# Turning token rows by DMA instead of on TensorE, with the norm's gains folded into the weights, in a hybrid SSD and RWKV-7 decoder layer

## The chip, the cores and the metric

The kernel runs on one core of one Trainium2 chip (trn2). The metric is the device time of one execution in microseconds. The core's engines each run their own queue of instructions: TensorE (PE in the profile, its weight loads PEld), VectorE (DVE), ScalarE (ACT), GpSimd (POOL) and SyncE (SP), which here only issues DMAs. An instruction waits at the head of its queue for the semaphores it needs, and everything behind it waits too.

## What is computed

One decoder layer over 2048 tokens of width 1024, in float32. Two groups of heads read the same normalised input:

```
xn   = RMSNorm(x) * pre_mix_norm
proj = xn @ w_in                       # 1024 -> 1544 (SSD) + 1792 (RWKV-7)
y_ssd, y_rwkv = ssd_mixer(...), rwkv7_mixer(...)
h = x + RMSNorm([y_ssd ; y_rwkv] @ w_out) * post_mix_norm
y = h + RMSNorm(ConvGLU(RMSNorm(h) * pre_ffn_norm)) * post_ffn_norm
```

The RWKV-7 mixer mixes each projected column with that of the token before (weight `mu`), forms a decay, keys, receptances and values, and runs a recurrence over tokens on a 64x64 state for each of eight heads:

```
sa = S @ a_t
S  = S * w_t + sa b_t^T + v_t k_t^T
y_t = S @ r_t
```

The SSD mixer passes its 1024 conv columns through a causal convolution of four taps, and does a chunked scan with chunks of 128 tokens.

## The kernel before

Three phases follow one another, each overlapping the next at its end: phase_R (the dense projections of RWKV-7 and of the SSD conv columns, the conv, and the RWKV-7 recurrence), phase_S (the SSD scan, the output projection, the first residual) and phase_F (the gated feed-forward network). The change lies nearly all in phase_R, with small parts in phase_S.

Phase_R works through 16 blocks of 128 tokens. The weights stay in SBUF for the whole phase: 14 tiles of 128 columns for RWKV-7 (`wr`) and 8 for the conv columns (`wc`). Each weight is scaled by 256 and split into a high and a low half of 16 bits (`load_w`, lines 280 to 295); the pattern SPLITS names who does it: "A" ScalarE or "G" GpSimd for the high half, "V" VectorE for the low one. The normalised tokens are split in the same way. A dense step (`dense`, line 210) is then 24 matmuls: eight slices of the 1024 inputs, and for each high by high, high by low and low by high.

Tokens arrive with tokens on the partitions, and the matmuls need them with the 1024 inputs on the partitions. The step `load` (line 312) does this for the next block. It has two halves. The first loads 512 KB of rows (`xin`), squares and sums them on ScalarE (line 190), forms the inverse root on GpSimd (lines 181, 182) and scales the rows on ScalarE (line 192). Each half then calls `flip_rows` (line 195): four TensorE transposes of 128x128 float32 into one PSUM bank (line 201), a VectorE multiply that empties the bank and applies `pre_mix_norm` (line 203), a ScalarE copy to the high half (line 206), and a VectorE subtraction for the low half (line 207). The bank has the tag "pt" with one buffer (in block 0 it is a buffer of "ms"). The result `xt` also goes to DRAM (`XN`, line 324) for phase_S.

The other steps of a block that the text names:

- `d.0` to `d.13` and `conv.0` to `conv.7`: the dense steps (lines 341 and 360), with what empties their PSUM banks: ScalarE copies (lines 353 to 355, 370), VectorE mixing (line 357), and for the conv a GpSimd bias (line 373), three taps on VectorE (line 378), a tanh and a product (lines 382, 383), and a store `XC` on SP (line 384).
- `low`, `keys`, `norm`, `receptance`: they make the decay and its cumulative sums (a VectorE scan with the mask `smask`, line 414), the keys and the scaled operands AR and BK.
- `gram.0`, `gram.1` (line 459): two sets of products of BK and AR, each into two banks of "ms", which VectorE masks into `G` (line 467). "ms" has two buffers and is shared with the small matmuls of `low`, `norm`, `transposed` and `values`.
- `solve` (line 471): the inverse of the unit triangular 32x32 blocks of G. Four DMAs carry the blocks to DRAM (`ATd`, line 479), four bring them back with one block per partition (`atl`, line 483), a chain of 62 small dependent VectorE instructions does forward substitution (lines 492, 495), four DMAs write the result (`XTd`, line 498) and four read it in its place (`XT`, line 504). All these are on SP.
- `merge.0`, `merge.1`, then `own`, `update` and `state` for each half block of 64 tokens, `transposed`, `values`, `gate`, `finish`: the recurrence proper. `merge.0` begins with two VectorE transposes of XT (`XW`, line 536) and the matmuls `pw` (line 543).

The order of TensorE's work is written out by hand in the tables FIRST (block 0), SECOND, PLAN (blocks 2 to 14) and LAST. In them `f.` is a step of the current block, `b.` of the block before, `a.` of the one before that, and `n.` of the next; so a block's dense steps, norm, gram and solve run in one round, and its merge and recurrence in the next. Only TensorE keeps this order as written (line 1498); the instructions of the other engines are put in order when the program is built, by a schedule that takes the order of the text as priority and its own estimate of the times. In PLAN, between the two grams and the next round, the order before is:

```
... f.conv.4 b.update.0 f.receptance f.gram.0 f.conv.5
f.gram.1 n.load.0 b.state.0 n.load.1 f.conv.6 b.own.1 f.conv.7 b.update.1 f.d.10 f.solve f.d.11 ...
```

Phase_S splits the weights of its z gate in four pieces of 1024 columns (`load_wz`, line 734).

Of the kernel before, what the change touches and what calls it, by code (L numbers as in the profile page):

```python
# [17 lines left out]
D = 1024  # L18
# [11 lines left out]
NC_S = 512  # L30
COLS = (
# [23 lines left out]
class Space:  # L55
# [22 lines left out]
    "cw cb mus omu w0h a0h ka5 kam tiny vr gnv gnr ss pnv pnr", "XT0 XT1 qs S0_0 S0_1 tS ysb yln tg",  # L78
# [3 lines left out]
    "wdt dtb Ab Db cst_s sng", "wst", "ws0", "ws1", "xt", "ws2", "ws3", "dv de dq ds dtt da nac", "sz", "th", "xbc", "R",  # L82
# [55 lines left out]
def load_consts(tc, K, pool, cst, par, rows, rows16):  # L138
    nc = tc.nc
    K.cst = pool.tile([P, NCONST - NC_S], F32, name="cst")  # L140
    nc.sync.dma_start(K.cst, cst[:, 0:NCONST - NC_S])
# [4 lines left out]
    for name, (a, b) in COFF.items():  # L146
        if b <= NCONST - NC_S:
            setattr(K, name, K.cst[:, a:b])
# [37 lines left out]
def norm_rows(tc, K, work, src, sfx, junk):  # L186
# [3 lines left out]
    nc.scalar.activation(junk, src.rearrange("p (a b) -> p a b", b=P), AF.Square, accum_out=ss)  # L190
    r = rsqrt_cols(tc, K, work, ss, 1, 1.0 / D, EPS, "pn")
    nc.scalar.activation(src, src, AF.Identity, scale=r[:, 0:1])


def flip_rows(tc, K, psp, pstag, src, g, dst, col, sfx, q):

    nc = tc.nc
    ps = psp.tile([P, 4, P], F32, name=f"pt{sfx}{q}", tag=pstag[0], bufs=pstag[1])
    for u in range(4):
        kt = 4 * q + u  # L200
        nc.tensor.transpose(ps[:, u, :], src[:, kt * P:(kt + 1) * P], K.ident)
# [1389 lines left out]
```

## Time and profile before

| | us |
|---|---|
| median of three runs | 2733.22 |
| the three runs | 2723.94, 2741.75, 2733.22 |
| the profiled execution | 2723.75 |
| its span, first to last instruction | 2722.0 |
| TensorE busy | 2500.4 (92%) |
| VectorE busy | 1951.3 (72%) |
| ScalarE busy | 1209.6 (44%) |
| GpSimd busy | 1251.6 (46%) |
| mean granted TensorE clock | 0.963 of full |

Phase_R's own work fills the first 954 us or so, with TensorE busy for 865 of them, and runs out beside phase_S from there on; phases S and F fill the rest. In the timeline a line gives the start, the length, the engine, the line of the program, the operation, the tile written and the tiles read, the shapes and the number of instructions merged; in brackets stands how long the engine had been idle before and what ended the wait. SPq is SP's queue of DMA issues. In a row of grouped instructions the last part is the idle time of the engine just before them and what ended it. In a row of stretches stand the stretch, its length, and for each of the engines TensorE, weight loads, VectorE, ScalarE and GpSimd the busy time, then the granted clock, the busy share of the DMA engines and GB/s. TensorE's clock is granted in full or by half, so a stretch shows a mean between 0.5 and 1.

### The profile page before, as it was taken

To read this page: it belongs to the slowest core of one execution; us is meant where nothing else is said; L and a number is where in the kernel's file an instruction comes from. 1 tells how busy PE (TensorE), PEld (TensorE's weight loads), DVE (VectorE), ACT (ScalarE), POOL (GpSimd) and SP (SyncE) were. 2 spreads that over 40 slices of the span, in tenths; PEclk is the share of its full clock that TensorE was granted. 3 is DMA by queue.
4 is the path that set the end of the run, shared out by engine and by line. 5 is a ranking of instruction groups with operands and counts; after the bars stand their busy time and mean duration, and the time that the engine had idled before them with its cause. 6 is when DMAs were issued, how large, how long until landed. Compare 5 with 4: busy or idle time off the path is not lost.

```text
span 2722.0 us, 54074 instructions
## 1 busy us (share of the span) xinstructions
PE 2500.4 (92%) x21468; PEld 1580.4 (58%) x21468; DVE 1951.3 (72%) x3649; ACT 1209.6 (44%) x2448; POOL 1251.6 (46%) x1348
## 2 busy tenths in 40 slices
PE   5999999999999979999987999898988999999998
PEld 4888888888888845555533444343433444444443
DVE  7778788888788655667777677787789734554457
ACT  5456555556555544444544543434344333122132
POOL 5334444344444443334468664746567523222234
PEclk8899999999999989999998999999998999999999
DMA  6221212211212343334454434343435633333243
GB/s 217 59 58 45 54 46 50 69 46 45 54 49 63 103 152 101 103 129 150 143 190 156 154 128 149 122 159 128 144 131 172 221 102 101 101 101 105 86 149 115
DMA packets 261279, 302.63 MB, mean 111 GB/s; under 512 B 133664, under 2 KB 168864, under 8 KB 257696
## 3 DMA queue, kind: packets, MB, share of 16 engines
q1 hardware_dynamic: 259440, 296.54, 34.1%
q8 instruction: 168, 2.75, 0.4%
q10 hardware_dynamic: 1584, 2.63, 0.3%
q14 instruction: 87, 0.71, 0.1%
HBM read 188.11 MB, written 110.99 MB: 110 GB/s over the span
## 4 chain that ended last, share of the span: by engine, by line
PE 40%; DVE 26%; POOL 13%; DMA 8%; issue 6%; ACT 4%; SPq 2%; POOLq 0%; DVEq 0%; ACTq 0%
PE u L1198 16%; PE d L1345 9%; PE d L216 3%; DVE ca L378 3%; DVE xl L495 3%; DMA HN<-hT 2%; PE c L216 2%; DVE tmp L492 2%; POOL fa L1103 2%; POOL us L1099 2%; DVE a L1235 2%; PE o L974 2%; PE l L1426 1%; POOL p L1263 1%; DMA XTd<-xl 1%
## 5 line engine op out<-in xcount | busy, mean ns | idle before, releaser
L1198 PE MATMUL u<-b,w 128*128 128x512 f16 x3696 | 818.7, 383 | 50.0 <-DVE C L1207 36.4
L1198 PEld LDWEIGHTS <-w 128*128 128x128 f16 x3696 | 365.0, 99 | 500.1 <-issue 76.2
L1345 PE MATMUL d<-dw,fa 128*128 128x512 f16 x1512 | 342.6, 386 | 17.2 <-DVE dw L167 16.5
L216 PE MATMUL d<-xt,wr 128*128 128x129 f16 x5376 | 325.7, 221 | 5.3 <-DVE xt L207 3.4
L216 PEld LDWEIGHTS <-wr 128*128 128x128 f16 x5376 | 315.8, 98 | 17.6 <-issue 13.3
L1345 PEld LDWEIGHTS <-fa 128*128 128x128 f16 x1596 | 158.7, 100 | 224.5 <-issue 37.2
L1207 DVE TENSOR_TENSOR C<-u,C 128x512 f32<-128x512 f32 x220 | 150.7, 685 | 187.2 <-PE u L1198 149.9
L216 PE MATMUL c<-xt,wc 128*128 128x131 f16 x3072 | 218.9, 233 | 8.7 <-ACT wc L291 4.6
L216 PEld LDWEIGHTS <-wc 128*128 128x128 f16 x3072 | 206.0, 104 | 22.3 <-issue 8.2
L1354 DVE TENSOR_TENSOR acc<-d,acc 128x512 f32<-128x512 f32 x212 | 140.0, 683 | 56.5 <-PE d L1345 55.2
L1235 DVE SCALAR_TENSOR_TENSOR p<-C,fpar,p 128x1024 f32<-128x1024 f32 x88 | 121.9, 1385 | 72.5 <-ACT p L1233 72.3
L378 DVE SCALAR_TENSOR_TENSOR ca<-rc,cw,ca 128x128 f32<-128x128 f32 x384 | 147.2, 417 | 35.0 <-POOL ca L373 32.0
L167 DVE SCALAR_TENSOR_TENSOR w<-us,w 128x512 f16<-128x512 f32 x132 | 120.0, 915 | 69.0 <-ACT w L166 67.9
L1102 ACT ACTIVATE fa<-p 128x512 f16<-128x512 f32 x132 | 79.6, 624 | 178.1 <-DVE p L1239 94.6
L1103 POOL TENSOR_TENSOR fa<-p,fa 128x512 f16<-128x512 f32 x120 | 151.7, 1274 | 3.1 <-ACT fa L1102 3.0
L495 DVE TENSOR_TENSOR xl<-xl,tmp 128x60 f32<-128x60 f32 (+24 forms) x465 | 137.2, 295 | 12.5
L492 DVE TENSOR_TENSOR tmp<-atl,xl 128x60 f32<-128x60 f32 (+24 forms) x465 | 117.8, 253 | 35.0 <-DMA atl<-ATd 25.0
L166 ACT ACTIVATE w<-us 128x512 f16<-128x512 f32 x132 | 80.5, 623 | 136.1 <-POOL us L1099 98.0
L373 POOL TENSOR_SCALAR ca<-rc,cw,cb 128x128 f32<-128x128 f32 x128 | 82.9, 656 | 117.0 <-ACT rc L370 94.0
L1235 DVE SCALAR_TENSOR_TENSOR a<-C,fpar,a 128x1024 f32<-128x1024 f32 x88 | 129.2, 1468 | 4.5 <-ACT a L1233 1.7
L1232 POOL COPY C<-fcarry 128x2 f32<-128x2 f32 x88 | 39.6, 452 | 157.3 <-ACT a L1233 77.2
L1237 POOL COPY fcarry<-C 128x2 f32<-128x2 f32 x88 | 33.4, 380 | 170.3 <-DVE C L1207 169.9
(320 smaller groups left out, 4562.0 us busy)
## 6 DMA issues: line engine op xcount, KB each, us to landing
UW<-w SPq DMA_DIRECT2D x154, 256.0 KB
w<-UW SPq DMA_DIRECT2D x154, 256.0 KB
us<-in_w_u_dram SPq DMA_DIRECT2D x44, 512.0 KB
DW<-dw SPq DMA_DIRECT2D x70, 256.0 KB
dw<-DW SPq DMA_DIRECT2D x56, 256.0 KB
hs<-HN SPq DMA_DIRECT2D x48, 256.0 KB
r<-in_w_d_dram SPq DMA_DIRECT2D x10, 1024.0 KB
xin<-in_x_dram SPq DMA_DIRECT2D x16, 512.0 KB
```

What stands on the lines that cost most here:

```text
L167: eng.scalar_tensor_tensor(out=lo, in0=src, scalar=scale, in1=hi, op0=ALU.mult, op1=ALU.subtract)
L216: nc.tensor.matmul(ps, w[:, a, kt, :], xt[:, kt, b, cols], start=n == 0, stop=n == 3 * KT - 1)
L373: G_.tensor_scalar(out=acc[:, q], in0=raw[:, q, 3:131], scalar1=cw[:, g + q, 3:4], scalar2=cb[:, g + q:g + q + 1], op0=ALU.mult, op1=ALU.add)
L378: V.scalar_tensor_tensor(out=acc[:, q], in0=raw[:, q, k:k + 128], scalar=cw[:, g + q, k:k + 1], in1=acc[:, q], op0=ALU.mult, op1=ALU.add)
L492: chain.tensor_tensor(out=tmp[:, :m, :n], in0=atl[:, j, j + 1:32].unsqueeze(1).to_broadcast([P, m, n]), in1=xl[:, :m, j:j + 1].to_broadcas ...
L495: chain.tensor_tensor(out=xl[:, :m, j + 1:32], in0=xl[:, :m, j + 1:32], in1=tmp[:, :m, :n], op=ALU.add)
L1103: eng.tensor_tensor(out=lo, in0=src, in1=hi, op=ALU.subtract)
L1198: nc.tensor.matmul(bk[at], self.w[i][:, u, k, :], self.half.b[i][:, k, v, :], start=start and n == 0, stop=n == 11, skip_group_check=True)
L1207: V.tensor_tensor(out=o, in0=ps, in1=a, op=ALU.add)
L1235: V.scalar_tensor_tensor(out=a, in0=c[:, 2 - d:1026 - d], scalar=cw[:, g, 2 - d:3 - d], in1=a, op0=ALU.mult, op1=ALU.add)
L1345: nc.tensor.matmul(ps, pairs[m].a[i][:, u, t * P:t * P + P], ws[n][m][:, v, :], start=new and m == 0 and u == v == 0, stop=m == N - 1 and ...
L1354: V.tensor_tensor(out=acc[j][:, t], in0=ps, in1=acc[j][:, t], op=ALU.add)
```

## The change

- **Transposes.** `norm_rows` and `flip_rows` become `split_rows`. The rows are scaled as before; ScalarE then copies them to a high half of 16 bits (1024 columns), GpSimd subtracts for the low half, written over the first half of the row's own buffer. Two DMA transposes on SP turn the halves into `xt`, whose layout is now half, slice, token. `load` is one step instead of two. The PSUM tag "pt" goes, and "ms" gets a third buffer.
- **Gains.** `pre_mix_norm` no longer multiplies the tokens. GpSimd multiplies each staged weight tile by it before the split (22 tiles); phase_S folds it into the dt weights by one VectorE multiply and into the z weights by the scale of their split, which is done in eight pieces instead of four.
- **Splits.** SPLITS is ('AV',): all high halves of the weights on ScalarE, all low ones on VectorE. Before, every fourth high half was GpSimd's.
- **Constants.** The mask of the scan is made on the chip in bfloat16, and the load of constants at the start shrinks from 1024 to 512 columns.
- **Order.** FIRST, SECOND and PLAN are rewritten. LAST and DRAIN stay.

```diff
-SPLITS = ('AV', 'AV', 'AV', 'GV')
+SPLITS = ('AV',)
...
 PLAN = """
-f.d.0 f.d.1 f.d.2 a.finish.1 b.values f.d.3 f.low.0 f.d.4 f.d.5 f.low.1 f.d.6 f.d.7 f.d.8 f.keys f.d.9 f.conv.0
-b.own.0 f.conv.1 b.merge.0 f.norm f.conv.2 b.merge.1 f.conv.3 f.conv.4 b.update.0 f.receptance f.gram.0 f.conv.5
-f.gram.1 n.load.0 b.state.0 n.load.1 f.conv.6 b.own.1 f.conv.7 b.update.1 f.d.10 f.solve f.d.11 f.d.12 f.transposed.0
-b.state.1 b.gate f.d.13 f.transposed.1 b.finish.0
+f.d.0 f.d.1 b.values f.low.0 f.d.2 a.finish.1 f.d.3 f.d.4 f.low.1 f.d.5 f.d.6 f.d.7 b.own.0 f.d.8 f.conv.0 f.keys
+f.d.9 f.conv.1 b.merge.0 f.norm f.conv.2 b.merge.1 f.conv.3 b.update.0 f.conv.4 f.receptance f.gram.0 f.gram.1 f.solve
+n.load f.conv.5 f.conv.6 b.state.0 f.conv.7 b.own.1 f.transposed.0 f.d.10 f.d.11 b.update.1 f.d.12 b.state.1 b.gate
+f.transposed.1 f.d.13 b.finish.0
...
+def split_rows(tc, K, work, src, hi, lo, sfx):
     nc = tc.nc
     ss = work.tile([P, 1], F32, name="ss" + sfx, tag="ss")
-    nc.scalar.activation(junk, src.rearrange("p (a b) -> p a b", b=P), AF.Square, accum_out=ss)
+    nc.scalar.activation(hi.bitcast(BF16), src, AF.Square, accum_out=ss)
     r = rsqrt_cols(tc, K, work, ss, 1, 1.0 / D, EPS, "pn")
     nc.scalar.activation(src, src, AF.Identity, scale=r[:, 0:1])
+    nc.scalar.activation(hi, src, AF.Copy)
+    nc.gpsimd.tensor_tensor(out=lo, in0=src, in1=hi, op=ALU.subtract)
...
             st = wk.tile([P, KT, P], F32, name=f"{name}{g}", tag=tag, bufs=2)
             nc.sync.dma_start(st, src[g])
+            G_.tensor_tensor(out=st, in0=st, in1=K.p_g_pre.unsqueeze(2).to_broadcast([P, KT, P]), op=ALU.mult)
...
             def ms(self, name):
-                return bank(name + self.sf, "ms", 2)
+                return bank(name + self.sf, "ms", 3)
...
+            def load(self):
                 it, sf = self.it, self.sf
+                xt = self.xt = wk.tile([P, 2, KT, 144], F16, name="xt" + sf, tag="xt", bufs=2)
...
+                xin = first if it == 0 else rows_of(it)
+                hi = wk.tile([P, D], F16, name="xh" + sf, tag="Pv")
+                lo = xin[:, 0:D // 2].bitcast(F16)
+                split_rows(tc, K, wk, xin, hi, lo, sf)
+                nc.sync.dma_start_transpose(xt[:, 0, :, 16:144], hi)
+                nc.sync.dma_start_transpose(xt[:, 1, :, 16:144], lo)
+                nc.sync.dma_start(XN[it // 2][:, :, :, (it % 2) * P:(it % 2) * P + P], xt[:, :, :, 16:144])
...
         for g in range(4):
             st = wk.tile([P, 2, 512], F32, name=f"sst{g}", tag="wst", bufs=2)
             pace(tc, K, nc.sync.dma_start(st, w_z[g]), "atl")
-            split_w(tc, W[g][:, :, 0], W[g][:, :, 1], st, V)
+            for k in range(2):
+                split_w(tc, W[g][:, k, 0], W[g][:, k, 1], st[:, k], V, gws[:, 2 * g + k:2 * g + k + 1])
```

More of the change, by code (lines that the diff above doesn't have):

```diff
@@ L30 @@
 NC_S = 512
+NCONST_R = 512
 COLS = (
@@ L139, in load_consts @@
     nc = tc.nc
-    K.cst = pool.tile([P, NCONST - NC_S], F32, name="cst")
-    nc.sync.dma_start(K.cst, cst[:, 0:NCONST - NC_S])
+    K.cst = pool.tile([P, NCONST_R], F32, name="cst")
+    nc.sync.dma_start(K.cst, cst[:, 0:NCONST_R])
     K.cst_dram = cst
@@ L146, in load_consts @@
     for name, (a, b) in COFF.items():
[L147 removed]
+        if b <= NCONST_R:
             setattr(K, name, K.cst[:, a:b])
@@ L183, in rsqrt_cols @@
     return r
-def norm_rows(tc, K, work, src, sfx, junk):
+def split_rows(tc, K, work, src, hi, lo, sfx):
     nc = tc.nc
     ss = work.tile([P, 1], F32, name="ss" + sfx, tag="ss")
-    nc.scalar.activation(junk, src.rearrange("p (a b) -> p a b", b=P), AF.Square, accum_out=ss)
+    nc.scalar.activation(hi.bitcast(BF16), src, AF.Square, accum_out=ss)
     r = rsqrt_cols(tc, K, work, ss, 1, 1.0 / D, EPS, "pn")
     nc.scalar.activation(src, src, AF.Identity, scale=r[:, 0:1])
[L195 to L201, printed above, removed]
-    half = src[:, 512 * q:512 * q + 512].rearrange("p (a b) -> p a b", b=P)
-    nc.vector.tensor_tensor(
-        out=half, in0=ps, in1=g[:, 4 * q:4 * q + 4].unsqueeze(2).to_broadcast([P, 4, P]), op=ALU.mult)
-    hi = dst[:, 4 * q:4 * q + 4, 0, col:col + P]
-    nc.scalar.activation(hi, half, AF.Copy)
-    nc.vector.tensor_tensor(out=dst[:, 4 * q:4 * q + 4, 1, col:col + P], in0=half, in1=hi, op=ALU.subtract)
+    nc.scalar.activation(hi, src, AF.Copy)
+    nc.gpsimd.tensor_tensor(out=lo, in0=src, in1=hi, op=ALU.subtract)
 def dense(tc, ps, w, xt, cols):
@@ L215, in dense @@
         for a, b in ((0, 0), (0, 1), (1, 0)):
-            nc.tensor.matmul(ps, w[:, a, kt, :], xt[:, kt, b, cols], start=n == 0, stop=n == 3 * KT - 1)
+            nc.tensor.matmul(ps, w[:, a, kt, :], xt[:, b, kt, cols], start=n == 0, stop=n == 3 * KT - 1)
             n += 1
@@ L269, in phase_R @@
         cb = small("cb", K.p_conv_b, 0.5, 0.0)
+        smask = wk.tile([P, 8, 64], BF16, name="smask")
+        G_.memset(smask, 1.0)
+        G_.memset(smask[:, :, 0:1], 0.0)
         tiny = wk.tile([P, 1], F32, name="tiny")
@@ L309, in ms @@
             def ms(self, name):
[L310 to L312 removed]
+                return bank(name + self.sf, "ms", 3)
+            def load(self):
                 it, sf = self.it, self.sf
[L314 to L324 removed]
+                xt = self.xt = wk.tile([P, 2, KT, 144], F16, name="xt" + sf, tag="xt", bufs=2)
+                if it == 0:
+                    V.memset(xt[:, :, :, 13:16], 0.0)
+                else:
+                    V.tensor_copy(xt[:, :, :, 13:16], blocks[it - 1].xt[:, :, :, 141:144])
+                xin = first if it == 0 else rows_of(it)
[5 more added lines that the diff above has]
+                nc.sync.dma_start(XN[it // 2][:, :, :, (it % 2) * P:(it % 2) * P + P], xt[:, :, :, 16:144])
             def begin(self):
@@ L658, in phase_R @@
         blocks = [Block(it) for it in range(iters)]
-        blocks[0].load(0)
-        blocks[0].load(1)
+        blocks[0].load()
         for g in range(14):
@@ L721, in phase_S @@
     V.tensor_scalar(out=sng, in0=K.p_ssd_norm, scalar1=WS, scalar2=None, op0=ALU.mult)
+    gws = wk.tile([P, 8], F32, name="gws")
+    V.tensor_scalar(out=gws, in0=K.p_g_pre, scalar1=WS, scalar2=None, op0=ALU.mult)
     ones3 = wk.tile([3, P], BF16, name="ones3")
@@ L736, in load_wz @@
         S.dma_start(sd, w_dt)
+        V.tensor_tensor(out=sd, in0=sd, in1=K.p_g_pre.unsqueeze(2).to_broadcast([P, KT, 8]), op=ALU.mult)
         split_w(tc, Wdt[:, :, 0], Wdt[:, :, 1], sd, V)
@@ L1492, in hybrid_layer @@
     dr = ctx.enter_context(tc.tile_pool(name="scratch", bufs=1, space=DRAM))
-    XN = [dr.tile([P, KT, 2, 256], F16, name=f"XN{i}") for i in range(8)]
+    XN = [dr.tile([P, 2, KT, 256], F16, name=f"XN{i}") for i in range(8)]
     XC = [dr.tile([P, 8, 256], F32, name=f"XC{i}") for i in range(8)]
```

42 lines of the change are left out of this document (15 added, 27 removed).

## The prediction

> **What bounds the kernel now.** I began with the page: its span, the busy times, and the slices.
>
> ```profile
> span 2722.0 us, 54074 instructions
> ...
> PE   5999999999999979999987999898988999999998
> ...
> DVE  7778788888788655667777677787789734554457
> ...
> PEclk8899999999999989999998999999998999999999
> ```
>
> TensorE sets the time nearly everywhere, so a change counts only as far as it gives TensorE less to do, fewer waits or a better clock. The change touches the recurrence phase, which the first 14 slices hold. Then I took busy time by stretch: the start, and twelve whole steady blocks, from one "pw" matmul (line 543, once per block) to the twelfth after it. The columns are TensorE, its weight loads, VectorE, ScalarE and GpSimd, then granted clock, DMA share and GB/s.
>
> ```profile
> 0.00:20.00 20.00, 6.95 (x53) 6.35 (x54) 10.85 (x24) 11.89 (x14) 6.66 (x14) 1.00 0.91 337
> 20.00:40.00 20.00, 15.13 (x217) 12.67 (x214) 16.16 (x23) 15.66 (x38) 11.37 (x9) 0.92 0.78 264
> 40.00:62.00 22.00, 11.11 (x136) 10.43 (x136) 18.96 (x19) 9.99 (x13) 16.32 (x8) 0.68 0.38 120
> ...
> 166.57:858.77 692.20, 650.55 (x10275) 601.70 (x10273) 572.21 (x1609) 390.41 (x904) 291.59 (x360) 0.97 0.21 52
> ```
>
> A block takes 692.20 / 12 = 57.68 us. TensorE is busy for 54.2 of them and idle for 3.47; VectorE is busy for 47.7, so it comes second. The waits of the same stretch say where TensorE's idle time goes (total, times, longest):
>
> ```profile
> PE pt L201 <- DVE xin L203: 28.6, 12, 2.6
> PE gr L463 <- DVE BK L447: 8.2, 10, 1.2
> ```
>
> Two thirds of it, 28.6 / 12 = 2.38 us per block, is one wait: the second set of token transposes (pt, line 201) has one PSUM bank, and waits until VectorE (line 203) has emptied it. The timeline of one block shows what follows:
>
> ```profile
> 513.65 0.69 PE L543 MATMUL pw<-XW,G 32*32 32x32 f32 x32
> ...
> 522.61 1.16 PE L463 MATMUL gr<-AR,BK 64*128 64x128 f32 x16 [1.19 <-DVE BK L447]
> 523.71 1.58 PE L216 MATMUL c<-xt,wc 128*128 128x131 f16 x24
> 525.40 1.75 PE L463 MATMUL gr<-AR,BK 64*128 64x128 f32 x16
> 527.09 0.66 PE L201 MATMUL pt<-cst,xin 128*128 128x128 f32 x4
> ...
> 531.80 1.08 PE L201 MATMUL pt<-cst,xin 128*128 128x128 f32 x4 [2.37 <-DVE xin L203]
> 532.68 2.80 PE L216 MATMUL c<-xt,wc 128*128 128x131 f16 x24
> ...
> 571.63 0.69 PE L543 MATMUL pw<-XW,G 32*32 32x32 f32 x32
> ```
>
> After the gap of 2.37 us the same 24 matmuls take 2.80 us instead of 1.58: the granted clock has fallen. A table of short stretches of that place shows it:
>
> ```profile
> 533.00:536.00 3.00, 3.00 (x43) 2.85 (x43) 2.58 (x5) 1.06 (x2) 0.94 (x3) 0.62 0.68 178
> 536.00:538.00 2.00, 2.00 (x37) 1.92 (x33) 0.90 (x5) 0.32 (x1) 0.00 (x0) 1.00 0.76 186
> ```
>
> The shorter wait of 1.19 us at 522.61 did no such thing: its matmuls at 523.71 ran at the full pace. Over the twelve blocks the clock of 0.97 costs 0.03 x 692.2 = 20.8 us, 1.73 per block.
>
> **The change, part by part. The transposes leave TensorE.** Eight per block go. A set of four takes 0.66 us at full clock (527.09), so 1.3 us with its neighbour; as consecutive sets overlap by a tenth, I take 1.2. With them go the wait of 2.38 and, if nothing else opens a gap as long, the 1.73 of slow clock: 5.3 us, and a block of 52.4.
>
> VectorE loses the eviction and the low halves, GpSimd gains one subtraction of 1024 columns, ScalarE swaps two copies of 512 columns for one of 1024:
>
> ```profile
> L207 DVE TENSOR_TENSOR xt<-xin,xt 128x512 f16<-128x512 f32 x24 | 19.5, 812 | 0.0
> ...
> L203 DVE TENSOR_TENSOR xin<-pt,par 128x512 f32<-128x512 f32 x24 | 16.4, 684 | 0.4
> ...
> L536 DVE STREAM_TRANSPOSE XW<-XT 32x256 f32<-32x256 f32 x24 | 10.4, 432 | 29.8 <-DMA XT<-XTd 29.7
> ```
>
> (19.5 + 16.4) / 12 = 3.0 us per block off VectorE. Nearest for GpSimd's new instruction are its other two-operand ones of 1024 columns, at 1917 ns (line 511, below); it has 692.2 - 291.6 us idle in the stretch, 33 per block, so 2 us lie beside TensorE. If that cover were gone they would delay the queue behind: the conv bias (line 373) and the scaling of BK (line 511).
>
> **Two DMA transposes per block, 256 KB each, on SP.** No such transfer is in this trace. Below, the queue's best: 186 GB/s (the stretch from 536 above) moves both in 2.8 us. Above, the solve's small pieces:
>
> ```profile
> 525.98 0.31 SPq L479 DMA_DIRECT2D ATd<-G  x1
> ...
> 526.83 4.63 SPq L479 DMA_DIRECT2D ATd<-G  x3
> 532.86 1.71 SPq L483 DMA_DIRECT2D atl<-ATd  x4
> ...
> 562.67 2.56 SPq L498 DMA_DIRECT2D XTd<-xl  x4
> ...
> 566.73 1.83 SPq L504 DMA_DIRECT2D XT<-XTd  x4
> ```
>
> Four XTd transfers of 32 KB go out from 562.67, and their reader starts at 566.73: 128 KB in 4.1 us, or 16 us for 512 KB. I take 5, nearer the lower end, since the source is contiguous rows as in the large loads. The halves should be ready near 528: the row scaling ends at 525.5, and a copy of 1024 columns and the subtraction follow.
>
> ```profile
> 524.31 1.15 ACT L192 ACTIVATE xin<-xin,pnr 128x1024 f32<-128x1024 f32 x1 [1.10 <-POOL pnr L182]
> ```
>
> The next block's first dense matmul is some 20 us away, so 5 us are hidden; the XN store, which now waits for the transposes on SP, holds whatever stands behind it for as long.
>
> **The order of steps.** The step solve moves ahead of conv.5 to d.10, and gram.1 stands right behind gram.0. First the price. A gram takes two "ms" banks and there are three, so the second matmul of gram.1 waits until VectorE has masked one bank. That is 0.68 us when VectorE is free, 1.5 when a conv group lies ahead, as here (gram.0 ends at 523.77, the first mask, half of the two, at about 525.3):
>
> ```profile
> 522.84 1.91 DVE L378 SCALAR_TENSOR_TENSOR ca<-rc,cw,ca 128x128 f32<-128x128 f32 x6 [0.28 <-POOL ca L373]
> 524.67 1.28 DVE L467 TENSOR_TENSOR G<-gr,cst 128x512 f32<-128x512 f32 x2
> ...
> 536.96 0.19 DVE L492 TENSOR_TENSOR tmp<-atl,xl 128x31 f32<-128x31 f32 x1 [1.35 <-DMA atl<-ATd]
> ...
> 569.77 0.43 DVE L536 STREAM_TRANSPOSE XW<-XT 32x256 f32<-32x256 f32 x1 [0.22 <-DMA XT<-XTd]
> ```
>
> I take 1.2, which makes 53.6, and no slow clock from it, as 1.19 brought none.
>
> Now the solve's own time. From the end of gram.1 (527.09) to XW (570.20) it needs 43.1 us. TensorE now takes 571.63 - 527.09 = 44.5 for what lies between, so nothing waits. Without the transposes, their wait and the slow clock that is 44.5 - 1.2 - 2.4 - 1.7, and conv.5 moves in (1.5): 40.7. Left as it is, the solve would be 2.4 us late at merge.0 in each block. But 25.6 of its 43.1 us are the chain of 62 small instructions on VectorE (536.96 to 562.6), whose busy time is only 17.3 per block:
>
> ```profile
> L495 DVE TENSOR_TENSOR xl<-xl,tmp 128x60 f32<-128x60 f32 (+24 forms) x372 | 113.2, 304 | 10.3
> ...
> L492 DVE TENSOR_TENSOR tmp<-atl,xl 128x60 f32<-128x60 f32 (+24 forms) x372 | 94.0, 253 | 27.2 <-DMA atl<-ATd 19.4
> ```
>
> Only TensorE's order is written by hand; the others are placed by the order of the text, and there the chain now comes before the work it was mixed with. Between no gain and the whole 8.3 us I take half, 4: the solve is in time, with 1.6 us over.
>
> **VectorE as the next limit.** 47.7 - 3.0 = 44.7 busy. Its remaining 57.68 - 47.7 = 10.0 us per block are waits, 2.5 of them for XT (29.8 / 12, above), and gaps between instructions. If all of these stayed, a block would take 54.7. Between 53.6 and 54.7 I take 54.1: 3.6 us per block. Of the 15 loads inside the blocks I count 13 with the full wait, the 12 quoted and the one for the last block behind the stretch; the first two give only their transposes.
>
> **The start.** GpSimd now multiplies each of 22 weight tiles by pre_mix, ahead of the split.
>
> ```profile
> L293 POOL TENSOR_SCALAR wc<-wct 128x1024 f16<-128x1024 f32 x2 | 8.9, 4446 | 5.3 <-DMA wct<-in_w_c_dram 5.3
> L293 POOL TENSOR_SCALAR wr<-wst 128x1024 f16<-128x1024 f32 x3 | 8.5, 2823 | 8.6 <-DMA wst<-in_w_r_dram 8.6
> ...
> L511 POOL TENSOR_TENSOR BK<-BK,Pi 128x1024 f32<-128x1024 f32 x1 | 1.9, 1917 | 3.2 <-PE gr L463 3.2
> ...
> 60.40 1.23 DVE L294 SCALAR_TENSOR_TENSOR wc<-wct,wc 128x1024 f16<-128x1024 f32 x1 [2.67 <-POOL wc L293]
> ...
> 72.29 1.57 PE L216 MATMUL c<-xt,wc 128*128 128x131 f16 x24
> ```
>
> 22 x 1.92 = 42 us come (line 511 has the same form), the five splits of line 293 go (17.4). Until 62 us GpSimd was busy for 34.4; now 34.4 - 17.4 + 42 + 4 for two low halves = 63, after some 6 us without input at the head: 69 to 70, and 2.3 more for the split. The last weight is ready near 72, not 61.6. Conv.7, which needs it, ran at 72.29, so the loss lies between 0 and 10; earlier groups come late as well, and block 0's rows now pass through two transposes. I take 8.
>
> The smaller constants, the mask built on the chip and the other XN layout (256-byte runs as before) I set at nothing: they lie under the first loads. The z weights are split in eight pieces instead of four, 1.5 us at most where TensorE already waits for them.
>
> **The sum:** 13 x 3.6 + 2 x 1.2 = 49 gained, 8 + 1.5 lost, 39.5 net. The profiled execution took 2723.75 us, its span 2722.0; it stands 9.5 under the median of 2733.22. From the median I forecast 2693 us.
>
> **Rivals.** *Clean:* no bank wait, the present 0.7 at gram gone as well, VectorE not in the way, start at its lower end. 13 x (5.3 + 0.7) + 2.4 = 80: 2653. For it: TensorE is at work 94% of the stretch. Against it: VectorE's 10 us of waits have other causes.
>
> *VectorE keeps its waits, the start costs its upper end:* 13 x 3.0 + 2.4 - 10 - 1.5 = 30, and where GpSimd's added work also stretches VectorE's instructions by 1 us per block, 17: 2716, no change. For it: line 378 averages 422 ns here and some 320 in the group at 522.84.
>
> *The transposes hold the solve (slower):* SP issues in order, and the halves are ready between 526 and 529, when ATd goes out. If both transposes and the waiting XN store are placed ahead of ATd or atl, the chain starts D later, and merge.0 stalls by 2.4 + D, less what the chain gains. With no gain a block is 56.0 + D, so it decides from D = 1.1 on, counting the start; with all of it, from about 9. At D = 8, the middle of 2.8 to 16, without the chain's gain, and with the slow clock back after so long a wait: 56.0 + 8 + 1.7 = 65.7, 13 x 8.0 + 9.5 - 2.4 = 111: 2844. Against it: SP is idle for most of a block, and atl waits for ATd anyway.
> The Trainium skill speaks for this rival (VectorE: DVE Perf Modes, The three transpose paths): it gives 1309 ns for a 128x128 tile by DMA against 390 ns on TensorE. Sixteen tiles in turn would be an estimated 20.9 us per block. Its page Advanced Engine Details and Errata (X-Bar Transpose) calls transposes as fast as other DMAs, which is my lower end; no run here shows either yet.
>
> **How the numbers follow.** A measurement tells about 1%, 27 us, from no change. Forecast 0.50 (own range 2672 to 2712), clean 0.18, VectorE 0.19, slower 0.13. Faster by over 1%: clean, and all but 0.04 of the forecast, 0.64; within 1%: 0.23; slower: 0.13. The range of 2645 to 2745 leaves out the lowest of clean (0.04) and nearly all of slower (0.11).
>
> **What would show it.** Right: blocks of about 54 us, no line 201, clock 1.00 over most blocks, waits of about 1 us between the two grams, a later conv.7 in block 0. Wrong: TensorE waiting at pw for XT (third rival), at the dense matmuls for xt (transposes far over 16 us), a clock still dropping once per block, or a start more than 10 us longer.

## The result and the profile after

The changed kernel takes 2743.15 us (median of 18 runs, 2738.43 to 2752.93), the kernel before 2729.66 us (18 runs) on the same chip: a ratio of 1.005, 95% interval 1.0039 to 1.006. The change costs 13 us where 40 were forecast as gained; the time lies within the 1% of "no change", just inside the upper end of the range. The profiled execution took 2740.43 us.

The page after, first the span, then TensorE, VectorE, GpSimd and the granted clock in 40 slices:

```profile
span 2738.6 us, 53831 instructions
...
PE   3789999999999988999996999998988899999998
...
DVE  7867787777877665667678678787789734554457
...
POOL 8434445454444353334558665747557523122234
PEclk7889999999999999999998999999999999999999
```

The loss shows in the first three slices (TensorE 3, 7 and 8 tenths busy; 5, 9 and 9 before), and the clock of the slices after the third is 9 nearly throughout. Stretches of the changed kernel, with the columns as in the prediction; the last is the twelve blocks from one pw to the twelfth after it:

```profile
0.00:20.00 20.00, 0.97 (x8) 0.83 (x9) 9.83 (x16) 8.84 (x10) 15.30 (x19) 1.00 0.95 324
20.00:40.00 20.00, 11.77 (x138) 11.35 (x137) 19.97 (x10) 7.41 (x10) 20.00 (x9) 0.83 0.63 202
40.00:62.00 22.00, 10.08 (x112) 9.11 (x111) 18.24 (x18) 12.47 (x31) 16.18 (x12) 0.66 0.32 105
62.00:85.00 23.00, 8.80 (x64) 6.87 (x65) 18.97 (x13) 9.26 (x13) 17.51 (x11) 0.50 0.28 92
...
203.38:875.81 672.43, 629.34 (x10178) 580.67 (x10176) 520.22 (x1560) 380.05 (x888) 320.46 (x372) 0.99 0.29 63
```

Two things are to be seen. At the start GpSimd and VectorE are both full from 20 to 40 us, and TensorE stands about half idle, and more, from 20 to 85 us, at a granted clock that falls from 0.83 to 0.50. In the steady stretch a block takes 672.43 / 12 = 56.04 us, 1.65 less than the 57.68 of before, not 3.6 less: TensorE is busy for 52.4 us of it (54.2 before; the transposes and part of the slow clock have gone), but idle for 3.6, as before (3.47). Its waits in those twelve blocks:

```profile
PE gr L457 <- DVE G L461: 16.8, 12, 1.4
PE pw L537 <- DVE XW L530: 10.0, 18, 2.0
PE c L204 <- ACT tr L349: 8.0, 10, 1.0
PE pS L600 <- ACT UV L583: 6.1, 7, 2.0
PE gr L457 <- DVE BK L441: 2.4, 11, 0.2
```

The wait at pt has gone, and five smaller ones, 43 us together, fill the idle time in its place. The ledger goes from the first pw, which stands in the round of block 1 and is called block 1's here, to the fifteenth, in the round of block 15. In the timeline of the kernel before:

```profile
107.67 0.24 PE L543 MATMUL pw<-XW,G 32*32 32x32 f32 x2
...
923.41 0.69 PE L543 MATMUL pw<-XW,G 32*32 32x32 f32 x32
```

In that of the changed kernel:

```profile
140.93 0.31 PE L537 MATMUL pw<-XW,G 32*32 32x32 f32 x2 [7.80 <-DVE XW L530]
...
939.92 0.69 PE L537 MATMUL pw<-XW,G 32*32 32x32 f32 x32
```

The start is 33.3 us longer, the fourteen blocks between are 16.7 us shorter, and from block 15 to the end both need the same (2722.0 - 923.41 = 1798.6 and 2738.6 - 939.92 = 1798.7). The forecast had 8 us lost at the start and 49 gained in the blocks: the start missed by 25 us, the blocks by 32.

### The profile page after: what moved, and what is told of

Its sections match the earlier page's. It is cut to its first block, busy times and chain, and to the rows that moved or that the text cites. A ratio compares the mean times of both kernels' runs of the same rounds, so it can differ in the third digit from the quotient of the medians.

```text
span 2738.6 us, 53831 instructions
## 1 busy us (share of the span) xinstructions
PE 2476.0 (90%) x21340; PEld 1557.8 (57%) x21340; DVE 1927.8 (70%) x3591; ACT 1209.0 (44%) x2443; POOL 1319.4 (48%) x1383
## 4 chain that ended last, share of the span: by engine, by line
PE 34%; DVE 23%; POOL 14%; DMA 10%; issue 7%; ACT 3%; SPq 3%; POOLq 0%; DVEq 0%; ACTq 0%
PE u L1195 15%; PE d L1342 9%; DVE tmp L486 4%; DVE xl L489 4%; POOL fa L1100 2%; DMA HN<-hT 2%; PE c L204 2%; PE o L971 2%; DMA atl<-ATd 1%; POOL us L1096 1%; DVE w L168 1%; POOL p L1260 1%; DMA XT<-XTd 1%; PE l L1423 1%; DVE ca L372 1%
## 5 line engine op out<-in xcount | busy, mean ns | idle before, releaser
L204 PE MATMUL d<-xt,wr 128*128 128x129 f16 x5376 | 338.2, 225 | 25.4 <-DMA xt<-xh 17.3
L204 PEld LDWEIGHTS <-wr 128*128 128x128 f16 x5376 | 324.4, 101 | 37.9 <-issue 28.3
L204 PE MATMUL c<-xt,wc 128*128 128x131 f16 x3072 | 209.4, 229 | 28.4 <-DVE wc L286 17.9
L204 PEld LDWEIGHTS <-wc 128*128 128x128 f16 x3072 | 193.0, 102 | 46.2 <-issue 21.8
L486 DVE TENSOR_TENSOR tmp<-atl,xl 128x60 f32<-128x60 f32 (+24 forms) x465 | 138.7, 298 | 40.6 <-DMA atl<-ATd 25.8
L168 DVE SCALAR_TENSOR_TENSOR w<-us,w 128x512 f16<-128x512 f32 x132 | 120.6, 921 | 56.9 <-ACT w L167 54.2
L372 DVE SCALAR_TENSOR_TENSOR ca<-rc,cw,ca 128x128 f32<-128x128 f32 x384 | 132.5, 389 | 26.1 <-POOL ca L367 25.6
L489 DVE TENSOR_TENSOR xl<-xl,tmp 128x60 f32<-128x60 f32 (+24 forms) x465 | 126.4, 272 | 11.0
L595 POOL TENSOR_TENSOR tS<-S,Pi 64x256 f32<-64x256 f32 x64 | 42.7, 666 | 164.3 <-DVE S L605 161.9
```

What stands on the lines that cost most here:

```text
L168: eng.scalar_tensor_tensor(out=lo, in0=src, scalar=scale, in1=hi, op0=ALU.mult, op1=ALU.subtract)
L204: nc.tensor.matmul(ps, w[:, a, kt, :], xt[:, b, kt, cols], start=n == 0, stop=n == 3 * KT - 1)
L372: V.scalar_tensor_tensor(out=acc[:, q], in0=raw[:, q, k:k + 128], scalar=cw[:, g + q, k:k + 1], in1=acc[:, q], op0=ALU.mult, op1=ALU.add)
L486: chain.tensor_tensor(out=tmp[:, :m, :n], in0=atl[:, j, j + 1:32].unsqueeze(1).to_broadcast([P, m, n]), in1=xl[:, :m, j:j + 1].to_broadcas ...
L489: chain.tensor_tensor(out=xl[:, :m, j + 1:32], in0=xl[:, :m, j + 1:32], in1=tmp[:, :m, :n], op=ALU.add)
```

## The experiments

Two theories were formed from this. A: the start loses its time to the 22 gain multiplies on GpSimd; the rival is block 0's rows, which now pass through two DMA transposes. B: the blocks gain little because of how the new order of steps, SP's queue and the solve stand to each other; the rival is that VectorE's own work holds them, wherever the transfers stand. Each experiment is told with its own ratio to the kernel before, measured beside it; the edits are shown shortened.

### The multiplies at the start

**e1**: the multiply is left out (and the gains with it).

```
-            G_.tensor_tensor(out=st, in0=st, in1=K.p_g_pre...to_broadcast([P, KT, P]), op=ALU.mult)
```

> The changed kernel without the 22 multiplications of the weight tiles by pre_mix (the gains are left out of the recurrence and conv columns; all else stays). Theory A: these multiplications on GpSimd make the start late. In the changed kernel the first pw of block 1 comes at 140.9 us, before the change at 107.7, so without them it should come at 105 to 115 and the time should fall by 25 to 35 us, to a ratio of about 0.993 to the kernel before. Rival B: the start is late because block 0's rows go through two transposing DMAs and through GpSimd, and because of the order of its steps; then pw stays near 135 and the ratio at 1.003 to 1.005.

2709.0 us, ratio 0.9928 (0.9901 to 0.9955), 34 us below the changed kernel; pw of block 1 at 107.86, where the kernel before has it.

**e4**: the other way round, the same 22 multiplies put into the kernel before (its gains then act twice).

> The kernel before with nothing but the 22 multiplications added on GpSimd (its own multiplication of the tokens stays, so the gains act twice). Theory A: they alone make the start late by 25 to 35 us, ratio 1.009 to 1.013. Rival B: without the transposing DMAs and the new order the multiplications hide as I had summed them: 0 to 10 us, ratio up to 1.004.

2767.09 us, ratio 1.0143 (1.0118 to 1.0167): 37 us more, pw of block 1 at 142.18. So the multiplies alone make a loss of that size, with the DMA transposes of block 0's rows (e1) or without them (e4). The transposes do show: the first dense matmul starts at 16.9 us in e1 and at 17.3 in the changed kernel, 11.6 before. But e1 has made that up by the first dense matmul of block 1 (73.7 us, 80.5 before).

**e9**: why do they cost so much? Either as a link (load, multiply, split) or by what they do to VectorE while both run. Here the product goes to a tile that nobody reads.

```
+            junk = wk.tile([P, KT, P], F32, name=f"j{name}{g}", tag="G", bufs=2)
-            G_.tensor_tensor(out=st, in0=st, ...)
+            G_.tensor_tensor(out=junk, in0=st, ...)
```

> The changed kernel with the 22 multiplies on GpSimd kept, but written to a tile that nobody reads, so that the splits do not wait for them (the gains are left out of the weights). It parts the two ways in which the multiplies can cost the start: as a link in the chain from a weight's load to its split, or by holding VectorE's splits up while both run. If they cost as a link: like the kernel without multiplies, 2705 to 2718 us, ratio 0.991 to 0.996, and the splits on VectorE stay near 1.4 us. If by holding VectorE up: 2735 to 2748 us, ratio 1.002 to 1.007, and the splits stay at 2 us and more. In between, both.

2739.18 us, ratio 1.0036 (1.0023 to 1.0049), pw of block 1 at 140.22. No split waits for a multiply here, and the loss is the same, so it does not need that link. (A thinner one stays: a staged tile takes the next load only when the multiply has read it, and SP waited 6.8 us for that in the first 105 us.) Groups of the first 105 us show what both engines do: the low halves of the weights (wr) on VectorE, and the multiplies (wst, wct) on GpSimd, in the changed kernel,

```profile
L286 DVE SCALAR_TENSOR_TENSOR wr<-wst,wr 128x1024 f16<-128x1024 f32 x14 | 29.3, 2124 | 9.7 <-ACT wr L283 9.7
...
L274 POOL TENSOR_TENSOR wst<-wst,par 128x1024 f32<-128x1024 f32 x14 | 35.6, 2574 | 1.4 <-DMA wst<-in_w_r_dram 1.4
L274 POOL TENSOR_TENSOR wct<-wct,par 128x1024 f32<-128x1024 f32 x8 | 17.0, 2133 | 0.1
```

in e1 without multiplies,

```profile
L285 DVE SCALAR_TENSOR_TENSOR wr<-wst,wr 128x1024 f16<-128x1024 f32 x14 | 18.0, 1304 | 6.6 <-ACT wr L282 6.4
```

and in e9:

```profile
L275 POOL TENSOR_TENSOR jwst<-wst,par 128x1024 f32<-128x1024 f32 x14 | 36.0, 2600 | 1.1 <-DMA wst<-in_w_r_dram 1.1
L287 DVE SCALAR_TENSOR_TENSOR wr<-wst,wr 128x1024 f16<-128x1024 f32 x14 | 34.3, 2498 | 6.0 <-ACT wr L284 6.0
```

The same VectorE instruction takes 1304 ns in the mean without the multiplies and 2498 beside them, and the multiply takes 2600 where the prediction had 1917. The shape and the data are the same; the two engines hold each other up. The Trainium skill states such a rule (SBUF — State Buffer, Who interferes with whom): VectorE with two SBUF inputs and GpSimd reading SBUF use one port pair, and the later one waits for the whole of the other's instruction. The rows agree with it.

**e2**: the multiplies on VectorE (`V.tensor_tensor` for `G_.tensor_tensor`), where the two kinds of work must add up.

> The changed kernel with the 22 multiplications on VectorE instead of GpSimd. In the changed kernel VectorE's low halves of the weights take 2124 ns in the mean instead of 1423, as they seem to wait for a GpSimd instruction under way and the other way round. If that mutual holding up is the cause of the late start (theory A1), 22 instructions of about 1.2 us on VectorE cost 26 us there and give back about as much stretching; pw of block 1 comes at 118 to 128, ratio 0.998 to 1.001. If it is only that each tile passes one more station and VectorE was full already (A2), pw comes at 140 or later and the ratio is 1.005 or more.

2724.45 us, ratio 0.9976 (0.9962 to 0.9989): 19 us better than on GpSimd, though VectorE now does both. A multiply takes 1.3 us there and the splits are back at 1.3; pw of block 1 comes at 122.88. The link is whole in this kernel and VectorE has 22 x 1.3 us more to do, and still more than half of the loss is gone: this speaks against the link more plainly than e9.

### Order, SP's queue and the solve

**e3**: the new bank wait between the two grams (1.4 us a block) is taken away by putting conv.5 between them, as before.

```
-f.receptance f.gram.0 f.gram.1 f.solve n.load f.conv.5 f.conv.6
+f.receptance f.gram.0 f.conv.5 f.gram.1 f.solve n.load f.conv.6
```

> The changed kernel with conv.5 put back between the two grams in SECOND and PLAN. In the changed kernel gram.1 waits 1.4 us for a masked bank in each block, 18 us over the steady stretch. Theory A (the wait is a loss of its own): it goes, blocks of 56.1 us become 54.8, and 13 of them give 15 to 18 us, ratio 0.999. Rival (the solve or VectorE sets the block, and TensorE would only wait elsewhere, at pw for XT): blocks stay within 0.5 us and the ratio at 1.003 to 1.005.

2843.95 us, ratio 1.0429 (1.0407 to 1.045): 101 us slower than the changed kernel, blocks of 64.2 us. The bank wait is gone, but TensorE now waits at pw for the solve, as its waits from 200 to 860 us say:

```profile
PE pw L537 <- DVE XW L530: 51.9, 22, 4.9
```

SP's queue in one block, whose second gram ended at 477.78, says why:

```profile
478.05 0.47 SPq L473 DMA_DIRECT2D ATd<-G  x1
478.62 1.28 SPq L316 DMA_TRANSPOSE xt<-xh  x1
480.30 1.24 SPq L317 DMA_TRANSPOSE xt<-xin  x1
481.63 2.18 SPq L473 DMA_DIRECT2D ATd<-G  x2
484.79 0.57 SPq L318 DMA_DIRECT2D XN<-xt  x1
485.41 1.09 SPq L221 DMA_DIRECT2D xin<-in_x_dram  x1
486.67 1.97 SPq L477 DMA_DIRECT2D atl<-ATd  x3
```

VectorE's first instruction of the chain there:

```profile
494.40 0.19 DVE L486 TENSOR_TENSOR tmp<-atl,xl 128x31 f32<-128x31 f32 x1 [4.71 <-DMA atl<-ATd]
```

The build places SP's transfers itself, and with the second gram later it puts both transposes ahead of the last two ATd, and XN and the load of the next rows ahead of the four atl. From the gram's end to the chain 16.6 us pass. That is the third rival's mechanism, in a kernel that differs from the changed one by one step of the order.

**e5**: e3 with the two transposes and XN made to follow the last atl transfer on SP.

```
+                for d in (dma_start_transpose(hi), dma_start_transpose(lo), dma_start(XN...)):
+                    if it:
+                        pace(tc, K, d, "atl")
```

> The kernel of e3 (conv.5 between the two grams, 2843.95 us) with one thing more: the two transposes and the write of XN are made to follow the last atl transfer on SP's queue, so SP carries ATd, atl, and only then the transposes, XN and the load of xin. Queue theory: e3 is slow because 2.5 us of transposes stand among the ATd transfers and XN and xin (1.7 us) ahead of the atl transfers, and the solve ends 4 to 5 us later in each block for it; then taking them away gives back 13 x 4 us or more, ratio at most 1.025 (2800 us or less), and TensorE's wait at pw for XW falls from 4.9 us to under 2. Rival, place of the gram: e3 is slow because the second gram comes 3.3 us later and the solve has no slack, whatever stands on SP; then 2830 to 2850 us, ratio 1.035 to 1.045.

2724.45 us, ratio 0.9978 (0.9961 to 0.9994): 120 us faster than e3. One block's SP queue, and the first instruction of its chain (second gram's end at 486.51):

```profile
486.79 1.68 SPq L476 DMA_DIRECT2D ATd<-G  x3
489.87 1.70 SPq L480 DMA_DIRECT2D atl<-ATd  x4
...
495.64 1.28 SPq L317 DMA_TRANSPOSE xt<-xh  x1
496.97 1.33 SPq L318 DMA_TRANSPOSE xt<-xin  x1
...
500.19 0.57 SPq L319 DMA_DIRECT2D XN<-xt  x1
```

```profile
496.47 0.18 DVE L489 TENSOR_TENSOR tmp<-atl,xl 128x31 f32<-128x31 f32 x1
```

The chain starts 10.0 us after the gram, 6.7 earlier than in e3, and a block takes 54.8 us.

**e6**: the same pacing alone, on the changed kernel.

> The changed kernel with the same one thing: transposes and the write of XN follow the last atl transfer on SP's queue. Queue theory: the solve ends late in the changed kernel too (TensorE waits 2.0 us for XW in ten of its blocks), and 2.5 us of transposes ahead of the third and fourth ATd transfer are the reason; then the blocks lose up to 2 us each: 2715 to 2730 us, ratio 0.995 to 1.000. Rival: the wait at pw comes from VectorE's chain, which other VectorE work stretches, and the transfers are hidden by that; then 2738 to 2748 us, ratio 1.003 to 1.007.

2738.35 us, ratio 1.0028 (1.0013 to 1.0043): the rival's answer by the time, but not by what the trace shows. First the changed kernel. Its SP queue, and the first instruction of its chain, in a block whose second gram ended at 439.82:

```profile
440.09 0.47 SPq L473 DMA_DIRECT2D ATd<-G  x1
440.66 1.29 SPq L316 DMA_TRANSPOSE xt<-xh  x1
442.05 1.03 SPq L473 DMA_DIRECT2D ATd<-G  x2
443.18 1.24 SPq L317 DMA_TRANSPOSE xt<-xin  x1
444.59 2.96 SPq L477 DMA_DIRECT2D atl<-ATd  x4
```

```profile
450.38 0.19 DVE L486 TENSOR_TENSOR tmp<-atl,xl 128x31 f32<-128x31 f32 x1 [2.09 <-DMA atl<-ATd]
```

From gram to chain 10.6 us pass. The first transpose held the second pair of ATd for about 1 us (its mask was ready at 440.93); the second lies in the time in which ATd lands. With pacing the chain starts 8.4 us after the gram in the mean of twelve blocks, against 10.6, and from 200 to 900 us TensorE's wait at pw fell from 10.0 to 2.9, those for tr and UV from 14.1 to 1.1. So the transposes had been in the way, by some 2 us a block. But gram.0's wait for BK rose from 2.7 to 15.5, and the granted clock of the stretch fell from 0.99 to 0.97. One block of e6 shows both:

```profile
375.30 1.38 PE L460 MATMUL gr<-AR,BK 64*128 64x128 f32 x18 [1.22 <-DVE BK L444]
378.13 2.07 PE L460 MATMUL gr<-AR,BK 64*128 64x128 f32 x14 [1.45 <-DVE G L464]
380.13 4.72 PE L204 MATMUL c<-xt,wc 128*128 128x131 f16 x48
```

In the changed kernel the same 48 matmuls took 2.97 us (at 384.77), behind one wait of 1.45 and one of 0.21. From 376 to 380 us e6's granted clock was 0.63, from 380 to 386 it was 0.68. From 200 to 860 us it fell after nine of e6's twelve pairs of waits; after the bank wait of 1.45 without the other, in the changed kernel, in two blocks of twelve. So what pacing won at pw went into a second wait and slower matmuls, and a block kept its length (56.2 us, 56.0 in the changed kernel). In e5, with conv.5 between the grams, the pair of waits does not arise and the clock is 1.00 from 200 to 900 us; that this is what makes e5 faster than e6 fits the sizes, but no run tests it by itself.

**e7 and e14**: the changed kernel with all of the old order (e7), and that order with the pacing (e14, for which the load of the rows stands behind the solve in the lists).

> The changed kernel with the kernel before's order of a block's steps (its four lists, the load of the rows at the place of the old first half): conv.5 stands between the grams, conv.4 between the solve and what follows it. It tells what the new order does for the new transposes. If the order is what protects the solve from the transposes on SP: like e3, 2800 to 2850 us, ratio 1.025 to 1.045. If the order matters little and e3 is a matter of its own: 2735 to 2750 us, ratio 1.002 to 1.007.

> The kernel of e7 (the changed kernel in the old order of steps, 2829.85 us) with its transposes and the write of XN behind the atl transfers; for that the load of the rows stands behind the solve in the lists. Queue theory: as in e3, most of e7's loss is the transposes' place on SP, and it comes back: 2715 to 2745 us, ratio 0.995 to 1.005. If the new order does something else that the DMA transposes need: 2770 to 2830 us, ratio 1.015 to 1.035.

e7 2829.85 us, 1.0353 (1.0325 to 1.038); e14 2740.47 us, 1.0039 (1.0021 to 1.0056). TensorE's wait at pw from 200 to 860 us in e7,

```profile
PE pw L537 <- DVE XW L530: 51.8, 20, 5.5
```

and in e14:

```profile
PE pw L540 <- DVE XW L533: 20.3, 21, 2.2
```

**e10**: the kernel before in the new order, with its own transposes.

> The kernel before with the changed kernel's order of a block's steps, its own TensorE transposes and splits kept. With the changed kernel's parts in the old order (2829.85 us) it fills the table of order by transposes. If the new order is better by itself (an earlier solve): 2700 to 2722 us, ratio 0.989 to 0.997. If it is only what the DMA transposes need, and costs the gram's wait for its bank (1.4 us a block): 2735 to 2755 us, ratio 1.002 to 1.009.

2775.25 us, ratio 1.017 (1.0153 to 1.0187), worse than either theory had it; its blocks take 61.1 us. This kernel has two "ms" banks where the changed one has three, and TensorE waits 1.7 us a block for one between the grams, 1.5 for the eviction of tr, and has a clock of 0.94. So e10 prices the new order with two banks; with three, on TensorE's transposes, it was not tried. Together, medians in us (the kernel before took 2729 to 2731 beside each):

| order of steps | TensorE transposes | DMA, placed by the build | DMA, behind atl |
|---|---|---|---|
| old | 2729.66 | 2829.85 | 2740.47 |
| new | 2775.25 | 2743.15 | 2738.35 |
| new, conv.5 between the grams | not tried | 2843.95 | 2724.45 |

The new order costs 45 us in the kernel before, with its two banks, and saves 87 where the DMA transposes are placed by the build: from the gram to the chain 16.1 us pass in e7's blocks and 10.6 in the changed kernel's, in the mean. Pacing gives that time back in the other two orders, and only then does conv.5 between the grams pay. So theory B is shown for the orders that leave the transposes ahead of atl. In the changed kernel pacing took waits away and gained next to nothing (5 us), as told at e6; that VectorE's own work holds its blocks is not shown there.

**e8**: the price of the transposes themselves: every pair issued twice. In the blocks the build puts the second pair behind atl.

> The changed kernel with every pair of transposes issued twice, into the same rows; the second pair stands behind the last atl transfer of the block on SP. It prices the transfers themselves: 2.5 us more of SP and twice the transposes' packets. If the transposes are hidden, as the prediction had it: 2740 to 2755 us, ratio 1.003 to 1.009, with some 3 us at most of it at the start, where the first dense product waits for them. If their traffic delays the solve or the rows of the next block: 1 to 2.5 us a block more, 2757 to 2780 us, ratio 1.010 to 1.018.

2743.35 us, ratio 1.0042 (1.0029 to 1.0056): 0.2 us more than once, which is nothing beside the spread. In the blocks the traffic is hidden, and so are 2.5 us of SP's time behind atl. In block 0 the second pair stands ahead of the first use and the first dense matmul starts at 22.0, not 17.3; that too is made up by the first dense matmul of block 1 (106.4, 110.5 in the changed kernel).

### What is left, and a better version

**e13**: e5 without the multiplies (gains left out): are the two causes the whole?

> The kernel of e5 (conv.5 between the grams, transposes and XN behind the atl transfers; 2724.45 us) without the 22 multiplies (the gains are left out of the weights). Two causes are held to make up the whole of the error: the start, where the multiplies cost 34 us, and the transposes' place on SP's queue, which with the order between the grams was worth 19 us. If they are the whole and add up: 2743 less 34 less 19, so 2690 us, ratio 0.983 to 0.988, near the 2693 us of the prediction. If something else holds the later phases or the blocks back once these two are gone: 2700 to 2712 us, ratio 0.989 to 0.994.

2687.24 us, ratio 0.9855 (0.9824 to 0.9886). The sum of the two single effects is 2743.15 - 34.1 - 18.7 = 2690.3. They add up within 3 us. That the time is within 6 us of the 2693 forecast is partly chance: pw of block 1 comes at 101.97, 5.7 us earlier than before where the forecast had the start 8 later, and the blocks take 55.0 where it had 54.1; and the order of the steps is no longer the forecast's.

**e11**: e5 with the multiplies on VectorE, which computes everything.

> The kernel of e5 (conv.5 between the grams, transposes and XN behind the atl transfers; 2724.45 us) with the 22 multiplies on VectorE. If start and blocks add up: 2724 less the 19 us that this was worth to the changed kernel, 2705 us, ratio 0.991. If the blocks are held by something that the start had covered: 2715 to 2725 us, ratio 0.995 to 0.998.

2713.13 us, ratio 0.9933 (0.9916 to 0.995): the best version that leaves nothing out, faster than both kernels. The edits do not quite add up (2743.15 - 18.7 - 18.7 = 2705.75); why, stays open.

**e12**: e5 with the gains folded into the splits, 128 columns an instruction.

> The kernel of e5 with the gains inside the splits: for each of a weight's eight column groups ScalarE writes the high half with the gain as its scale and VectorE the low half with the gain as its scalar, 128 columns an instruction, and no multiply stands by itself. If the start is held by VectorE's and GpSimd's busy time: 2695 to 2705 us, ratio 0.986 to 0.991 (the kernel without multiplies gained 34 us on the changed one). If 176 small instructions on ScalarE, at some 0.25 us each, hold it instead: 2708 to 2720 us, ratio 0.992 to 0.996.

2723.53 us, ratio 0.9974 (0.9961 to 0.9987), no better than e5. The two halves of the weights wr in its first 105 us, and TensorE's longest wait there:

```profile
L278 ACT ACTIVATE wr<-wst,gwr 128x128 f16<-128x128 f32 x112 | 33.1, 384 | 0.0
L279 DVE SCALAR_TENSOR_TENSOR wr<-wst,gwr,wr 128x128 f16<-128x128 f32 x112 | 32.6, 363 | 2.5 <-ACT wr L278 2.3
```

```profile
PE d L204 <- ACT GL L345: 35.0, 1, 35.0
```

A piece takes 384 ns by itself, but they overlap: 112 keep ScalarE busy for 33.1 us and the 64 of wc for 18.8, 0.295 us each against the 0.25 expected. That is 52 us, and TensorE waits for an eviction (line 345) that stands behind them.

**e15**: e11 with the low half of the rows on VectorE instead of GpSimd.

> The kernel of e11 (2713.13 us: paced, conv.5 between the grams, multiplies on VectorE) with the low half of each block's rows made on VectorE instead of GpSimd, where one took 2.2 to 4.3 us. If GpSimd's long instructions hold VectorE up by about their own time in the blocks too: VectorE gains what it takes on, and the time falls by 0 to 1 us a block: 2698 to 2712 us, ratio 0.988 to 0.993. If VectorE is the bound in the blocks and only its own work counts, 1.2 us a block more: 2714 to 2732 us, ratio 0.994 to 1.001.

2731.04 us, ratio 1.0003 (0.9989 to 1.0018), 17.9 us worse than e11. The moved instruction (duration minimum, median, maximum):

```profile
L195 DVE TENSOR_TENSOR xin<-xin,xh x16: 1218/1226/1304, 10.6 to 878.8; 128x1024 f16<-128x1024 f32 x16
```

16 x 1.23 = 19.6 us of VectorE cost 17.9 us of time, but that these are nearly equal is chance. A block takes 57.1 us, 2.3 more than e11's 54.8, while the first pw comes 2.7 us earlier and the phases after the fifteenth took 4.9 less in the profiled execution. So the instruction costs more than its own length in a block, although VectorE is busy for only 80% of the stretch from 200 to 860 us (530.46 of 660). Part of it is where it stands: VectorE waits for ScalarE's copy before it (7.0 us in all, 14 times), and the chain starts 12.9 us after the gram, 10.1 in e11. In the blocks GpSimd's 2.1 us, and whatever they hold up, are the cheaper.

## Why the prediction was wrong, step by step

It failed at two places: the start, where 8 us were counted and 33.3 came, and the blocks, where 3.6 us each were counted as gained and 1.65 came. The steps that made these terms follow one by one.

**The transposes leave TensorE: right, but the slow clock was counted as gone whole.** The wait at line 201 has gone. But TensorE's busy time fell by 1.8 us a block, not by the 2.9 of the sum (1.2 for the transposes, 1.73 for the clock), and the clock of the stretch rose from 0.97 to 0.99, not to 1.00. New waits slow it: from 200 to 860 us it fell after one of 2.05 us at pS (342.9), one of 2.05 at pw (541.6), and two of the bank waits of 1.45 (719.4 and 832.2). These 1.1 us are the larger part of the 1.9 by which a block missed the forecast (56.0 against 54.1); how much of them is the clock and how much the matmul groups that start afresh after a new wait is not parted.

**Two DMA transposes at 5 us, hidden: right.** In e5 the first is issued at 495.64 and XN, which waits for both, at 500.19: 4.6 us. The Trainium skill's 1309 ns a tile (VectorE: DVE Perf Modes, The three transpose paths), an estimated 20.9 us a block, does not hold here; its other statement (Advanced Engine Details and Errata, X-Bar Transpose), as fast as other DMAs, is nearer. In the changed kernel's block 0 the second one is used 4.3 us after its issue, and e1, whose first dense matmul is as late, shows that block 0 as a whole loses nothing by it:

```profile
15.01 1.25 SPq L317 DMA_TRANSPOSE xt<-xin  x1
...
19.30 2.98 PE L204 MATMUL d<-xt,wr 128*128 128x129 f16 x26 [1.77 <-DMA xt<-xin]
```

**The bank wait, 1.2 us a block: right**, 16.8 / 12 = 1.4. The slow clock that was not to come from it did come in two blocks of twelve, and in nine of twelve in e6.

**The chain tightens by 4 us: wrong.** In the block shown it ran from 450.38 to 475.67, 25.3 us against 25.6, busy 17.9 of them; the solve from gram.1 to XW took 44.1 us, not 39. In the mean of twelve blocks the chain took 25.2 us, 25.4 before. Other VectorE work is still mixed in. Without the 4 us the prediction's own sum has the solve late, and 0.8 us a block of it shows at pw. The forecast left 2.8 us of idle time a block (3.47 - 2.38, the bank wait of 1.2, and 0.5 for VectorE); 3.6 came: 1.4 for the bank, 0.8 at pw, 0.7 for tr, 0.5 for UV and 0.2 at gram.0. The solve's lateness at pw is as large as the difference. Which engine's work makes the waits for tr and UV stays open.

With both terms twelve blocks gave 19.8 us and not 12 x 3.6 = 43. The first one took 3.5 us more than before (62.4 against 58.9) instead of 1.2 less. Part of that is only pw's place, which the new order moves forward in this block's round; from this block's first dense matmul to the next block's 66.3 us pass, 63.6 before. e1, without the multiplies, takes longer still there; why stays open. e5 and e13, with conv.5 between the grams and the solve's transfers kept free, came to 54.8 and 55.0 us a block.

**VectorE as the next limit: not shown.** Its idle time did not stay at 10.0 us a block but rose to (672.43 - 520.22) / 12 = 12.7. e15 shows, in another kernel, that work added to it in the blocks costs more than its own length.

**The start, 8 us: wrong.** It was 33.3 to pw, 30 to block 1's first dense matmul (110.5, 80.5 before): the largest miss of a single term. The step that failed took the multiplies by GpSimd's durations alone (22 x 1.92) and left VectorE's splits at theirs. In the changed kernel the 22 multiplies took 53.1 us, not 42, and the 22 low halves 43.2, where e1's took 27.9. Had both engines' work been added where it overlaps, the last weight would have come 22 x 1.3 = 29 us after the predicted 72, at 101. It came there:

```profile
101.11 1.98 PE L204 MATMUL c<-xt,wc 128*128 128x131 f16 x22 [3.12 <-DVE wc L286]
```

That the sum meets the time is partly chance: GpSimd was busy for 77.0 and VectorE for 80.6 of those 101 us, and the rest they waited. As a warning the sum would have served.

**The z weights, 1.5 us: nothing is seen of it** (the ends of both kernels agree to 0.1 us); no run tests it by itself.

**The rivals.** The third (the transposes hold the solve) did not decide the changed kernel: in the block shown the chain starts 10.6 us after the gram against 9.9 before, 0.7, under its point of 1.1. But e6 shows that without the transposes in the way it starts some 2 us earlier in the mean. Its mechanism is real: with D = 6.7 it made e3, and pacing undid it. The second (VectorE keeps its waits, GpSimd stretches VectorE) had the right mechanism in the wrong place: the stretching decided the start. Clean (2653) was not reached by any run; the nearest is e13, 2687 us, which leaves the gains out.

## What to carry to other kernels

Before moving work to GpSimd, add its time to that of VectorE wherever both run two-input operations on SBUF in the same stretch, as here; ask whether the engine is idle together with VectorE, not by itself. When transfers are added to a queue whose order the build chooses, fix the place of those that nobody waits for behind those that somebody does: here that decided 120 us, and it decided whether another edit gained or lost. Where a wait goes and the block does not shrink, look at the granted clock and at the waits that took its place before naming the engine that holds the block.

## What the runs showed of the hardware

- GpSimd and VectorE, fp32 operations with two inputs of 1024 columns: 1.30 us on VectorE without GpSimd's multiplies (e1), 2.50 beside them (e9), where the multiplies took 2.60. An instruction of 512 columns (tk, line 434) took 2.38 us beside a multiply and 0.69 in a later block.
- A DMA transpose of 128 x 1024 16-bit elements takes 1.24 to 1.33 us of SP in the blocks shown; two in turn are done 4.6 us after the first issue (e5), and a second pair in every block cost no time that can be told from the spread (e8).
- ScalarE: 1.05 us for a copy of 1024 columns with a constant scale, 0.384 for 128 columns with a scale per partition. In a row of such pieces each keeps it busy for 0.295 (e12), so eight cost 2.4 us, more than twice the whole.
- TensorE's granted clock from 200 to 860 us: it fell after nine of eleven waits of 2.25 to 2.4 us (the kernel before), after two of twelve bank waits of 1.36 to 1.45 (changed kernel), and after nine of twelve pairs of 1.2 and 1.45 that stand 1.4 us apart (e6). After such a pair 48 matmuls took 4.72 us, 2.97 at full clock.
